# Fifteen weight blocks of a layer's input projection by Strassen's scheme (seven products of quarter blocks) in float32 sums

## The chip, the cores and the metric

The kernel runs on one core of a Trainium2 chip. Its engines are TensorE (PE; its weight loads, PEld, run beside its matmuls), VectorE (DVE), ScalarE (ACT), GpSimd (POOL) and SyncE (SP, which issues the DMA transfers). Each engine works through its own list of instructions in order. The metric is the device time of one execution in microseconds.

## The reference

One decoder layer on 1024 tokens of width 1024, all in float32, and a final norm:

```
h = rms_norm(x, norm_w);  proj = h @ w_in
z, xbc, dt_raw, pool_u, pool_gate, qkv, sb_gate, merge = split(proj)
y_ssm  = mamba2_branch(z, silu(causal_dwconv(xbc)), dt_raw, ...) @ w_proj_ssm
y_pool = pool_branch(pool_u, pool_gate, ...) @ w_proj_pool
y_sb   = stick_breaking_branch(qkv, sb_gate) @ w_proj_sb
x = x + (sum of sigmoid(merge_i) * y_i) @ w_out;  return rms_norm(x, final_norm_w)
```

## The kernel before, in words

Everything rests on products of h with blocks of 256 weight columns. A float32 operand is split into two float32r parts, `hi` (a cast, on ScalarE) and `lo` (the rest, a subtraction on Vector), and a product is three matmuls: hi·hi, hi·lo and lo·hi. A block in the transposed form (`gemm_b`, L148) is 2 column tiles of 128 times 2 token halves of 512, each 8 k-tiles times 3 matmuls of 512 columns: 96 matmuls. In the token form (`gemm_a`, L157) it is 8 token tiles times 24 matmuls of 256 columns. `hT[k]` holds the hi and lo of h's k-th tile for all 1024 tokens. `PLAN` is the order in which the blocks' weights are loaded (`load_half`, two 512 KB halves, through two `raw` buffers) and split (`split_half`).

`conv_part` is the first phase. Block ("x", 0) is computed while h is normed and transposed; ("x", b) for b up to 9 feeds the causal convolution: ScalarE writes the first tap from PSUM to `cacc` (L442), Vector adds three more taps from PSUM (L447), ScalarE takes a sigmoid (L450), GpSimd multiplies (L451), and a DMA stores the result. ("z", 0) with the dt columns follows ("x", 1); the short chain of dt (L378 to L418) is spread over the blocks after it. Then come ("g", 0) to ("g", 2), a SiLU gate for attention.

`attention_part` runs 64 units (8 head pairs, 2 heads, 4 pairs of query tiles). A unit's scores go PE, ACT (two sigmoids), DVE (scan L610, product L611), PE (transposes), ACT and DVE (split), PE (`av`). Between a unit's steps, TensorE is given fill: weight blocks of later work from the list `ATT_FILL`, spread over a pair's units by `share`. For six of the eight pairs the fill is three blocks: `vz` and `qk` of the next pair and one more (("g", 3), ("z", 1) to ("z", 3), ("m", 0), ("m", 1)); the first and the last pair have two. `merge_gen` (("m", i)) only copies its product out. The order of PE is written out by hand in attention, and that of PE, DVE, POOL and ACT in the first phase: there an engine that waits holds up all that stands behind it in the program. The scan, pool and merge phases follow.

## Time and profile before

| what | us |
|---|---|
| median of 3 runs (2081.27 to 2083.81) | 2081.63 |
| the profiled execution | 2080.79 |
| its span | 2079.0 |
| PE busy in the span | 2048.6 |
| DVE, ACT, POOL busy | 1203.2, 904.6, 348.9 |

The profiled execution's own time is its span and what lies around it (1.79 us). Busy time is the union of an engine's instructions, with matmul ends modelled; the share of an engine that does not bound a stretch says little about it.

### The profile page before, as it was taken

Reading aid. Unit: us, or ns where it says so; the run is one execution under the profiler, and the core shown is the slowest. Engines: PE = TensorE matmul, PEld = TensorE weight load, DVE = VectorE, ACT = ScalarE, POOL = GpSimd, SP = SyncE. Lnnn points to the kernel's source line nnn. Section 1 sums busy time; section 2 is a strip of 40 time slices with the busy share of each in tenths; the row PEclk is TensorE's granted clock in tenths of the full one; section 3 lists DMA queues with packets and bytes.
Section 4 is the critical chain, followed back from the end, with each engine's and each line's share of the span. In section 5 each row is a group of like instructions: output and inputs, shape, how many; then the busy total and the mean of one; then the engine's idle time right before and its main releaser. Section 6 shows DMA issues by size and latency. Waiting matters only on the chain.

```text
span 2079.0 us, 29567 instructions
## 1 busy us (share of the span) xinstructions
PE 2048.6 (99%) x11480; PEld 1751.9 (84%) x11480; DVE 1203.2 (58%) x1635; ACT 904.6 (44%) x1841; POOL 348.9 (17%) x415
## 2 busy tenths in 40 slices
PE   8999999999999999999999999999999999999998
PEld 6988889979899998888877877788888888888898
DVE  6466632676666776766774777773545424425333
ACT  5243322555555555555555666763322323323131
POOL 3112200021111111111112344430000002221000
PEclk9999999999999999999999999999999999999999
DMA  4323232112121212212215566654222625433232
GB/s 155 110 94 104 101 104 92 44 54 75 48 72 47 67 57 62 72 41 79 59 51 172 187 203 198 208 163 146 86 76 78 218 96 189 149 101 109 81 133 82
DMA packets 111677, 221.49 MB, mean 107 GB/s; under 512 B 9393, under 2 KB 59313, under 8 KB 111537
## 3 DMA queue, kind: packets, MB, share of 16 engines
q1 hardware_dynamic: 111536, 219.60, 32.4%
q8 instruction: 91, 1.49, 0.3%
q14 instruction: 50, 0.40, 0.1%
HBM read 162.15 MB, written 57.41 MB: 106 GB/s over the span
## 4 chain that ended last, share of the span: by engine, by line
PE 92%; DVE 4%; ACT 2%; issue 1%; DMA 1%; POOL 0%; SPq 0%; DVEq 0%; POOLq 0%; ACTq 0%
PE mm L148 34%; PE mmx L148 24%; PE mm L157 13%; PE mmx L157 4%; PE av L651 3%; PE yd L874 3%; PE tr L628 2%; DVE om L610 2%; PE z L601 1%; PE z L602 1%; PE yo L877 1%; PE st L880 1%; PE pp L755 1%; DVE be L611 1%; PE xp L858 1%
## 5 line engine op out<-in xcount | busy, mean ns | idle before, releaser
L148 PE MATMUL mm<-hT,w 128*128 128x512 f32 x2808 | 717.7, 401 | 3.1 <-DVE hT L345 2.8
L148 PEld LDWEIGHTS mm<-hT,w 128*128 128x128 f32 x2808 | 510.8, 188 | 115.6 <-issue 15.3
L129 DVE TENSOR_TENSOR w<-raw,w 128x1024 fp32r<-128x1024 f32 x142 | 207.7, 1463 | 149.6 <-ACT w L128 149.3
L157 PE MATMUL mm<-w,hT 128*128 128x256 f32 x2112 | 283.9, 286 | 1.2 <-ACT qb L545 1.2
L148 PE MATMUL mmx<-hT,w 128*128 128x512 f32 x1224 | 281.5, 389 | 0.0
L148 PEld LDWEIGHTS mmx<-hT,w 128*128 128x128 f32 x1224 | 229.7, 188 | 47.7
L157 PEld LDWEIGHTS mm<-w,hT 128*128 128x128 f32 x2112 | 263.4, 191 | 2.2 <-ACT qb L545 1.7
L148 PE MATMUL mmx<-x,w 128*128 128x512 f32 x1008 | 230.9, 389 | 0.0
L148 PEld LDWEIGHTS mmx<-x,w 128*128 128x128 f32 x1008 | 189.2, 188 | 39.3
L610 DVE TENSOR_TENSOR_SCAN om<-om,zero 128x128 f32<-128x128 f32 (+7 forms) x128 | 174.4, 1363 | 69.6 <-ACT om L605 69.0
L128 ACT CAST w<-raw 128x1024 fp32r<-128x1024 f32 x142 | 148.6, 1049 | 65.8 <-PE mmx L148 32.3
L630 ACT CAST attT<-tr 128x512 fp32r<-128x512 f32 (+2 forms) x224 | 98.4, 439 | 147.0 <-PE tr L628 79.3
L631 DVE TENSOR_TENSOR attT<-tr,attT 128x512 fp32r<-128x512 f32 (+2 forms) x224 | 111.0, 496 | 76.1 <-ACT attT L630 74.1
L605 ACT ACTIVATE om<-z 128x128 f32<-128x128 f32 (+2 forms) x192 | 92.8, 495 | 78.3 <-PE z L604 75.7
L148 PE MATMUL mm<-x,w 128*128 128x512 f32 x528 | 122.5, 390 | 0.0
L148 PEld LDWEIGHTS mm<-x,w 128*128 128x128 f32 x528 | 98.8, 188 | 21.5 <-ACT x L978 0.7
L1002 ACT ACTIVATE gt<-gt 128x1024 f32<-128x1024 f32 x32 | 34.0, 1062 | 184.0 <-DMA gt<-d_gate 181.3
L851 POOL TENSOR_TENSOR E<-E,cbm 128x1024 f32<-128x1024 f32 x32 | 76.3, 2385 | 161.4 <-issue 121.9
L611 DVE TENSOR_TENSOR be<-be,om 128x128 f32<-128x128 f32 (+7 forms) x128 | 96.9, 757 | 10.4
L1011 POOL TENSOR_TENSOR acc<-acc,gt 128x512 f32<-128x512 f32 x32 | 45.9, 1435 | 293.0 <-DVE gt L1010 293.0
L608 ACT ACTIVATE be<-z 128x128 f32<-128x128 f32 (+2 forms) x192 | 93.0, 498 | 0.1
L628 PE MATMUL tr<-cm,be 128*128 128x128 f32 x576 | 89.5, 273 | 0.5 <-DVE be L611 0.5
(194 smaller groups left out, 2515.6 us busy)
## 6 DMA issues: line engine op xcount, KB each, us to landing
raw<-in_wblk SPq DMA_DIRECT2D x148, 512.0 KB, 3.9
E<-d_act SPq DMA_DIRECT2D x32, 512.0 KB, 4.3
gt<-d_gate SPq DMA_DIRECT2D x32, 512.0 KB, 3.8
d_gate<-mg SPq DMA_DIRECT2D x24, 512.0 KB, 3.4
d_x<-csg SPq DMA_DIRECT2D x16, 512.0 KB, 2.7
xi<-d_x SPq DMA_DIRECT2D x32, 256.0 KB, 3.2
zs<-d_z SPq DMA_DIRECT2D x32, 256.0 KB, 2.8
d_ssm<-yt SPq DMA_DIRECT2D x32, 256.0 KB, 3.1
```

The lines of the kernel that those rows point to most:

```text
L128: nc.scalar.copy(hi, raw)
L129: nc.vector.tensor_tensor(out=lo, in0=raw, in1=hi.bitcast(F32), op=ALU.subtract)
L148: T.matmul(ps, w(a, k, ct * P, ct * P + P), mov(b, k, half * 512, half * 512 + 512), start=n == 0, stop=n == 23)
L157: T.matmul(ps, sta(a, k, tok * P, tok * P + P), w(b, k, 0, ncol), start=n == 0, stop=n == 23)
L605: A.activation(om[:, c0 : c0 + n], z[:, 0:n], AF.Sigmoid, scale=-0.125)
L608: A.activation(be[:, c0 : c0 + n], z[:, 0:n], AF.Sigmoid, scale=0.125)
L610: V.tensor_tensor_scan(out=rev, data0=rev, data1=self.zero.broadcast_to((P, L)), initial=1.0, op0=ALU.mult, op1=ALU.add)
L611: V.tensor_tensor(out=be[:, 0:L], in0=be[:, 0:L], in1=om[:, 1 : L + 1], op=ALU.mult)
L628: T.transpose(tr[:, c : c + P], b[:, (2 * jc + j) * P : (2 * jc + j + 1) * P], self.ident)
L630: A.copy(at[:, 0, sl], tr[:, sl])
L631: V.tensor_tensor(out=at[:, 1, sl], in0=tr[:, sl], in1=at[:, 0, sl].bitcast(F32), op=ALU.subtract)
L851: G.tensor_tensor(out=E, in0=E, in1=cbm[:, hg // 2].unsqueeze(1).broadcast_to((P, 8, P)), op=ALU.mult)
```

## The change

For fifteen blocks (`SEVEN`: x3 to x9, g0 to g3, m0 to m3) the product of the 1024 x 256 block A (transposed) with h is taken as a 2 x 2 product of quarters: A's halves over k and over columns, h's halves over k and over tokens. Winograd's form of Strassen's scheme needs seven quarter products, four sums of weight quarters (s1 to s4, per block, on GpSimd) and four of h (t1 to t4, once, on GpSimd and Vector, kept in `tt` and, for t1, in the upper token half of `hT[0]` to `hT[3]`, whose old content is parked in DRAM and brought back at the end), and seven sums of products. A quarter product is 4 k-tiles times 3 matmuls: 84 matmuls in a block for 96. Products five to seven are accumulated onto the PSUM banks of products one, three and four.

("g", 3) and ("m", 0) to ("m", 3) move from the fill of attention to the first phase; five pairs keep two fill blocks, the fourth gets ("z", 1), the last ("z", 2) and ("z", 3). ("z", 0) moves ahead of ("x", 1). The convolution of x3 to x9 reads SBUF, not PSUM, and stands in the next block's steps (`before`), as the gate of g0 to g3 does; the splits of the next block's quarters (`seven_prep`) stand there too.

```diff
-    extra = [("g", 3)] + [("z", i) for i in range(1, 4)] + [("m", i) for i in range(4)]
     order = [[("vz", p + 1), ("qk", p + 1)] for p in range(7)]
-    for p in range(1, 7):
-        order[p].insert(0, extra.pop(0))
-    return order + [extra]
+    order[3].insert(0, ("z", 1))
+    return order + [[("z", 2), ("z", 3)]]
+
+SEVEN = [("x", 3), ("g", 0), ("x", 4), ("m", 0), ("x", 5), ("g", 1), ("x", 6), ("m", 1), ("x", 7), ("g", 2), ("x", 8), ("m", 2), ("x", 9), ("g", 3), ("m", 3)]
...
+    for i in range(3):
         part(("x", i), OFF_X + 256 * i)
-        if i == 1:
+        if i == 0:
             part(("z", 0), OFF_Z + 1024)
-    for i in range(3):
-        part(("g", i), OFF_SG + 256 * i)
+    for kind, i in SEVEN:
+        part((kind, i), {"x": OFF_X, "g": OFF_SG, "m": OFF_M}[kind] + 256 * i)
...
+    def seven_prep(self, b):
+
+        nc = self.nc
+        G, A, V = nc.gpsimd, nc.scalar, nc.vector
+        assert self.wnext == 2 * b
+        self.wnext += 2
+        r0, r1 = (self.raw.pop(2 * b + i).rearrange("p (a b) -> p a b", b=256) for i in range(2))
+        a11, a21, a12, a22 = r0[:, :, 0:P], r0[:, :, P:256], r1[:, :, 0:P], r1[:, :, P:256]
+        t0 = self.wpool.tile([P, 2, 4, 256], F32R, tag="w", name=f"w{2 * b}")
+        t1 = self.wpool.tile([P, 2, 4, 256], F32R, tag="w", name=f"w{2 * b + 1}")
+        t2 = self.wspool.tile([P, 2, 4, 384], F32R, tag="ws", name=f"ws{b}")
+        s1, s2, s3, s4 = (self.s32pool.tile([P, 4, P], F32, tag="s32", name=f"s{i}", bufs=4) for i in range(4))
+        self.wseven[b] = {
+            "a11": lambda a, k: t0[:, a, k, 0:P],
+            "s2": lambda a, k: t0[:, a, k, P:256],
+            "s3": lambda a, k: t1[:, a, k, 0:P],
+            "s1": lambda a, k: t1[:, a, k, P:256],
+            "a12": lambda a, k: t2[:, a, k, 0:P],
+            "a22": lambda a, k: t2[:, a, k, P:256],
+            "s4": lambda a, k: t2[:, a, k, 256:384],
+        }
+
+        def split(t, c0, c1, src):
+            A.copy(t[:, 0, :, c0:c1], src)
+            V.tensor_tensor(out=t[:, 1, :, c0:c1], in0=src, in1=t[:, 0, :, c0:c1].bitcast(F32), op=ALU.subtract)
+
+        G.tensor_tensor(out=s1, in0=a21, in1=a22, op=ALU.add)
+        G.tensor_tensor(out=s2, in0=s1, in1=a11, op=ALU.subtract)
+        G.tensor_tensor(out=s3, in0=a11, in1=a21, op=ALU.subtract)
+        G.tensor_tensor(out=s4, in0=a12, in1=s2, op=ALU.subtract)
+        split(t0, 0, P, a11)
+        yield
+        split(t2, 0, 256, r1)
+        self.load_half()
+        self.load_half()
+        yield
+        split(t0, P, 256, s2)
+        yield
+        split(t1, 0, P, s3)
+        yield
+        split(t1, P, 256, s1)
+        yield
+        split(t2, 256, 384, s4)
+
...
+    def seven_operands(self, pool):
+
+
+        nc = self.nc
+        G, V = nc.gpsimd, nc.vector
+        self.tt = {i: pool.tile([P, 2, 4, 512], F32R, name=f"tt{i}") for i in (2, 3, 4)}
+        self.park = self.dram.tile([P, 4, 2, 512], F32, name="d_b12")
+        self.t1 = []
+        lo, hi = slice(0, 512), slice(512, 1024)
+        f = lambda t, part, sl: t[:, part, sl].bitcast(F32)
+
+        def tmp(name):
+            return self.s32pool.tile([P, 512], F32, tag="s32", name=name, bufs=4)
+
+        for k in range(4):
+            a, c = self.hT[k], self.hT[4 + k]
+            nc.sync.dma_start(out=self.park[:, k], in_=a[:, :, hi].bitcast(F32))
+            t1 = pool.tile([P, 512], F32, name=f"t1_{k}")
+            d, e = tmp("td"), tmp("te")
+            G.tensor_tensor(out=d, in0=f(a, 0, hi), in1=f(a, 0, lo), op=ALU.subtract)
+            G.tensor_tensor(out=t1, in0=f(a, 1, hi), in1=f(a, 1, lo), op=ALU.subtract)
+            V.tensor_tensor(out=t1, in0=t1, in1=d, op=ALU.add)
+            self.t1.append(t1)
+            G.tensor_tensor(out=e, in0=f(c, 0, hi), in1=t1, op=ALU.subtract)
+            V.tensor_tensor(out=e, in0=e, in1=f(c, 1, hi), op=ALU.add)
+            self.t_split(2, k, e)
+            yield
+            d = tmp("td")
+            G.tensor_tensor(out=d, in0=f(c, 0, lo), in1=e, op=ALU.subtract)
+            V.tensor_tensor(out=d, in0=d, in1=f(c, 1, lo), op=ALU.add)
+            self.t_split(4, k, d)
+            d, e = tmp("td"), tmp("te")
+            G.tensor_tensor(out=d, in0=f(c, 0, hi), in1=f(a, 0, hi), op=ALU.subtract)
+            G.tensor_tensor(out=e, in0=f(c, 1, hi), in1=f(a, 1, hi), op=ALU.subtract)
+            V.tensor_tensor(out=d, in0=d, in1=e, op=ALU.add)
+            self.t_split(3, k, d)
+            yield
+
+    def t_split(self, i, k, src):
+        hi, lo = self.tt[i][:, 0, k], self.tt[i][:, 1, k]
+        self.nc.scalar.copy(hi, src)
+        self.nc.vector.tensor_tensor(out=lo, in0=src, in1=hi.bitcast(F32), op=ALU.subtract)
+
+    def seven_first(self):
+
+        nc = self.nc
+        for k in range(4):
+            hi, lo = (self.hT[k][:, i, 512:1024] for i in range(2))
+            nc.scalar.copy(hi, self.t1[k])
+            nc.vector.tensor_tensor(out=lo, in0=self.t1[k], in1=hi.bitcast(F32), op=ALU.subtract)
+
+    def seven_last(self):
+        for k in range(4):
+            self.nc.sync.dma_start(out=self.hT[k][:, :, 512:1024].bitcast(F32), in_=self.park[:, k])
+
...
+    def seven_block(self, name, before, prep):
+
+        nc = self.nc
+        A, V, T = nc.scalar, nc.vector, nc.tensor
+        w = self.wseven.pop(BLK[name])
+        h = self.hT
+        mov = {
+            "b11": lambda b, k: h[k][:, b, 0:512],
+            "b21": lambda b, k: h[4 + k][:, b, 0:512],
+            "b22": lambda b, k: h[4 + k][:, b, 512:1024],
+            "t1": lambda b, k: h[k][:, b, 512:1024],
+            "t2": lambda b, k: self.tt[2][:, b, k],
+            "t3": lambda b, k: self.tt[3][:, b, k],
+            "t4": lambda b, k: self.tt[4][:, b, k],
+        }
+
+        def product(ps, a, b, first):
+            n = 0
+            for k in range(4):
+                for i, j in ((0, 0), (0, 1), (1, 0)):
+                    T.matmul(ps, w[a](i, k), mov[b](j, k), start=first and n == 0, stop=n == 11, skip_group_check=not first)
+                    n += 1
+
+        def step(i):
+            for f in before.get(i, ()):
+                f()
+            next(prep, None)
+
+        def add(out, ps, other):
+            V.tensor_tensor(out=out, in0=ps, in1=other, op=ALU.add)
+
+        c = [self.c_pool.tile([P, S + 4], F32, tag="cacc", name="cx") for _ in range(2)]
+        q = lambda i, j: c[i][:, 3 + 512 * j : 515 + 512 * j]
+        pu = self.stage("pu")
+        p1, u2, u3 = pu[:, 0:512], pu[:, 512:1024], q(0, 1)
+        x = self.mm()
+        product(x, "a11", "b11", True)
+        A.copy(p1, x)
+        step(0)
+        y = self.mm()
+        product(y, "s2", "t2", True)
+        add(u2, y, p1)
+        step(1)
+        z = self.mm()
+        product(z, "s3", "t3", True)
+        add(u3, z, u2)
+        step(2)
+        v = self.mm()
+        product(v, "s1", "t1", True)
+        add(q(1, 1), v, u3)
+        step(3)
+        product(x, "a12", "b21", False)
+        A.copy(q(0, 0), x)
+        step(4)
+        product(z, "a22", "t4", False)
+        add(q(1, 0), z, u2)
+        step(5)
+        product(v, "s4", "b22", False)
+        add(q(0, 1), v, u2)
+        step(6)
+        return c
+
...
+    def seven_x(self, b, c):
+
+        nc = self.nc
+        accs = []
+
+        def first():
+            for ct in range(2):
+                col = 2 * b + ct
+                nc.gpsimd.memset(c[ct][:, 0:3], 0.0)
+                acc = self.c_pool.tile([P, S], F32, tag="csg", name="acc", bufs=2)
+                cw = lambda k: self.conv_w[:, col, k : k + 1]
+                nc.scalar.activation(acc, c[ct][:, 3 : 3 + S], AF.Identity, scale=cw(3), bias=self.conv_b[:, col : col + 1])
+                for k in range(3):
+                    nc.vector.scalar_tensor_tensor(acc, c[ct][:, k : k + S], cw(k), acc, op0=ALU.mult, op1=ALU.add)
+                accs.append(acc)
+
+        def second(ct):
+            col = 2 * b + ct
+            sg = c[ct][:, 0:S]
+            nc.scalar.activation(sg, accs[ct], AF.Sigmoid)
+            nc.gpsimd.tensor_tensor(out=sg, in0=sg, in1=accs[ct], op=ALU.mult)
+            dst = self.d_x[col // 4][:, col % 4] if col < 16 else self.d_bc[:, col - 16]
+            nc.sync.dma_start(out=dst, in_=sg)
+
+        return {0: [first], 2: [lambda: second(0)], 3: [lambda: second(1)]}
+
...
+            self.zd = self.sb(zctx, "zd_sb", 1).tile([P, 2, 8, 288], F32R, name="zd")
             norm = self.norm_in(self.sb(nctx, "n_sb", 3), pps)
             for _ in range(3):
                 next(norm)
+            self.drain(self.conv_gen(0, pool, norm))
+            nctx.close()
+            self.zd_open(dpool)
             dt = self.dt_part(dpool)
-            for b in range(10):
-                self.drain(self.conv_gen(b, pool, norm if b == 0 else None))
-                if b == 0:
-                    nctx.close()
-                    self.zd_open(ctx, dpool)
-                else:
-                    next(dt, None)
-            for b in range(3):
-                self.drain(self.g_gen(b))
+            next(dt)
+            zctx.close()
+            tpool = self.sb(ctx, "t_sb", 1, "right")
+            self.s32pool = self.sb(ctx, "s32_sb", 1, "right")
+            sums = self.seven_operands(tpool)
+            for i, _ in enumerate(self.conv_gen(1, pool)):
+                next(sums, None)
+                if i > 1:
+                    next(sums, None)
+                if i % 2:
+                    next(dt)
+            self.wseven = {}
+            for i, _ in enumerate(self.conv_gen(2, pool)):
+                next(sums, None)
+                if i == 1:
+                    self.drain(sums)
+                    self.drain(dt)
+                    dctx.close()
+                    self.wspool = self.sb(ctx, "ws_sb", 2)
+                    prep = self.seven_prep(BLK[SEVEN[0]])
...
+
+            def halves():
+                for _ in range(2):
+                    self.split_half()
+                    yield
+
+            before = {}
+            for i, (kind, b) in enumerate(SEVEN):
+                prep = self.seven_prep(BLK[SEVEN[i + 1]]) if i + 1 < len(SEVEN) else halves()
+                before = make[kind](b, self.seven_block((kind, b), before, prep))
+            for i in sorted(before):
+                for f in before[i]:
+                    f()
+            self.seven_last()
         self.dump("bc", self.d_bc)
```

On GpSimd, in the first phase before, only the 20 multiplications of the convolution stand between the weight splits of the start and attention:

```order
L126 TENSOR_TENSOR w_426<-raw_215,w_426 128x512 x2
L126 TENSOR_TENSOR w_437<-raw_222,w_437 128x512 x2
L451 TENSOR_TENSOR csg<-csg,cacc 128x1024 x20
L592 MEMSET om 128x1 x2
L625 MEMSET attT 128x2x128
```

Now, during ("x", 1), the sums of h for the second, and then the third, pair of k-tiles stand between them (td, te: scratch; t_1, t_2: t1's tiles; of the trunk `csg` one row is left here):

```order
L213 TENSOR_TENSOR td<-hT_103 128x512
L214 TENSOR_TENSOR t_1_926<-hT_103 128x512
L217 TENSOR_TENSOR te<-hT_107,t_1_926 128x512
L222 TENSOR_TENSOR td<-hT_107,te 128x512
L226 TENSOR_TENSOR td<-hT_107,hT_103 128x512
L227 TENSOR_TENSOR te<-hT_107,hT_103 128x512
L663 TENSOR_TENSOR csg<-csg,cacc 128x1024
L213 TENSOR_TENSOR td<-hT_104 128x512
L214 TENSOR_TENSOR t_2_982<-hT_104 128x512
L217 TENSOR_TENSOR te<-hT_108,t_2_982 128x512
L222 TENSOR_TENSOR td<-hT_108,te 128x512
L226 TENSOR_TENSOR td<-hT_108,hT_104 128x512
```

Each of these sums stands between steps of Vector and ScalarE that it waits for or that wait for it, and the multiplication of `csg` (L663) stands in the same list. On Vector, an x block before was a split, and three taps from PSUM after each product:

```order
L129 TENSOR_TENSOR w_1064<-raw_910,w_1064 128x1024
L430 COPY cacc<-cols 128x3
L447 SCALAR_TENSOR_TENSOR cacc<-mm,cols,cacc 128x512 x3
L447 SCALAR_TENSOR_TENSOR cacc<-mm,cols,cacc 128x510
L447 SCALAR_TENSOR_TENSOR cacc<-mm,cols,cacc 128x511
L447 SCALAR_TENSOR_TENSOR cacc<-mm,cols,cacc 128x512
```

Now the six taps of an x block (L324, SBUF to SBUF) stand at the start of the next block's list, ahead of its splits (L174) and its sums of products (L278; pu and cx on the left are u2, then u3 and the four quarters):

```order
L324 SCALAR_TENSOR_TENSOR acc<-cx,cols,acc 128x1024 x6
L174 TENSOR_TENSOR w_1649<-raw_1537,w_1649 128x4x128
L278 TENSOR_TENSOR pu<-mmx,pu 128x512
L174 TENSOR_TENSOR ws_1651<-raw_1539,ws_1651 128x4x256
L278 TENSOR_TENSOR cx<-mmx,pu 128x512
L174 TENSOR_TENSOR w_1649<-s_1653,w_1649 128x4x128
L278 TENSOR_TENSOR cx<-mmx,cx 128x512
L174 TENSOR_TENSOR w_1650<-s_1654,w_1650 128x4x128
L174 TENSOR_TENSOR w_1650<-s_1652,w_1650 128x4x128
L278 TENSOR_TENSOR cx<-mmx,pu 128x512
L174 TENSOR_TENSOR ws_1651<-s_1655,ws_1651 128x4x128
L278 TENSOR_TENSOR cx<-mmx,pu 128x512
```

The sums of products, which PSUM banks wait for, moved behind the taps and between the splits. On TensorE the dt product, which stood behind ("x", 3):

```order
L148 MATMUL mmx<-hT_108,w_978 128x512 x3
L148 MATMUL mmx<-hT_109,w_978 128x512 x3
L400 MATMUL mmx<-adt,cm 128x256
L404 MATMUL mm<-adt,cm 128x256
L148 MATMUL mm<-hT_102,w_1064 128x512 x3
L148 MATMUL mm<-hT_103,w_1064 128x512 x3
```

now stands right behind ("x", 1), two blocks sooner after the product that it comes from:

```order
L361 MATMUL mm<-hT_109,w_582 128x512 x3
L610 MATMUL mm<-adt,cm 128x256
L616 MATMUL mmx<-adt,ones 128x256
L361 MATMUL mmx<-hT_102,w_774 128x512 x3
L361 MATMUL mmx<-hT_103,w_774 128x512 x3
```

## Rows read from the trace of the kernel before

**Rows 1.** The page, part 1: busy us, share of the span, instructions.
```profile
PE 2048.6 (99%) x11480; PEld 1751.9 (84%) x11480; DVE 1203.2 (58%) x1635; ACT 904.6 (44%) x1841; POOL 348.9 (17%) x415
```

**Rows 2.** Chain that ended last, in order: start us, us, what.
```profile
37.24 16.36 PE mmx L148 x72
...
336.10 23.03 PE mm L157 x192
359.13 21.79 PE mm L148 x96
```

**Rows 3.** Timeline of 48 to 52.5 us, Vector and GpSimd: start us, us, what.
```profile
48.39 2.42 POOL L451 TENSOR_TENSOR csg<-csg,cacc 128x1024 f32<-128x1024 f32 x1 [3.55 <-ACT csg L450]
49.02 2.32 DVE L447 SCALAR_TENSOR_TENSOR cacc<-mmx,cols,cacc 128x510 f32<-128x510 f32 x3 [3.13 <-ACT cacc L442]
...
51.25 0.28 DVE L357 CAST zd<-wdt_raw 128x256 fp32r<-128x256 f32 x1
...
51.57 0.42 DVE L358 TENSOR_TENSOR zd<-wdt_raw,zd 128x256 fp32r<-128x256 f32 x1
```

**Rows 4.** Timeline of 118 to 165 us, a convolution stretch.
```profile
121.96 1.28 ACT L380 ACT_TABLE_LOAD   x1
...
125.43 1.75 DVE L388 RECIPROCAL dt_w<-dt_w 128x256 f32<-128x256 f32 x1 [0.33 <-ACT dt_ln L384]
...
150.48 1.23 DVE L129 TENSOR_TENSOR w<-raw,w 128x1024 fp32r<-128x1024 f32 x1 [0.51 <-ACT w L128]
...
158.99 2.40 POOL L451 TENSOR_TENSOR csg<-csg,cacc 128x1024 f32<-128x1024 f32 x1 [9.84 <-ACT csg L450]
...
159.83 2.65 DVE L129 TENSOR_TENSOR w<-raw,w 128x1024 fp32r<-128x1024 f32 x1 [3.31 <-ACT w L128]
```

**Rows 5.** Timeline of 1225 to 1262 us, GpSimd, a scan stretch.
```profile
1223.70 2.38 POOL L851 TENSOR_TENSOR E<-E,cbm 128x1024 f32<-128x1024 f32 x1 [4.41 <-issue]
1226.03 1.50 POOL L886 TENSOR_TENSOR S<-S,dt_all 128x512 f32<-128x512 f32 x1
```

**Rows 6.** The same stretch, Vector.
```profile
1225.83 0.80 DVE L887 TENSOR_TENSOR y<-y,xk 128x512 f32<-128x512 f32 x1
```

**Rows 7.** Groups by line and form: line, engine, names, shapes, count | busy us, mean ns | idle.
```profile
L781 ACT COPY mg<-mm 128x512 f32<-128x512 f32 x48 | 28.0, 584 | 38.4 <-PE mm L148 38.2
L447 DVE SCALAR_TENSOR_TENSOR cacc<-mm,cols,cacc 128x512 f32<-128x512 f32 x36 | 27.0, 750 | 5.0 <-ACT cacc L442 3.7
...
L450 ACT ACTIVATE csg<-cacc 128x1024 f32<-128x1024 f32 x20 | 21.2, 1062 | 47.1 <-DVE cacc L447 29.7 <-DVE cacc L430 17.4
...
L442 ACT ACTIVATE cacc<-mmx,cols 128x509 f32<-128x509 f32 x14 | 10.9, 776 | 45.6 <-PE mmx L148 45.5
...
L1016 DVE TENSOR_TENSOR mg<-acc,mg 128x512 fp32r<-128x512 f32 x16 | 10.3, 687 | 5.3 <-ACT mg L1015 5.3
...
L734 DVE SCALAR_TENSOR_TENSOR u<-s,u 128x1024 f32<-128x1024 f32 x8 | 9.8, 1226 | 0.3
```

**Rows 8.** Timeline of 1728 to 1746 us, GpSimd.
```profile
1729.12 1.29 POOL L1011 TENSOR_TENSOR acc<-acc,gt 128x512 f32<-128x512 f32 x1 [1.54 <-DVE gt L1010]
```

**Rows 9.** Busy us (instructions) of each engine in two stretches of attention.
```profile
core 0: us, PE busy (x) PEld busy (x) DVE busy (x) ACT busy (x) POOL busy (x), PEclk, DMA share, GB/s
...
870.20:966.40 96.20, 95.19 (x601) 83.31 (x600) 65.37 (x91) 51.72 (x114) 13.69 (x32) 1.00 0.20 61
...
1055.40:1091.20 35.80, 33.60 (x191) 27.41 (x191) 26.48 (x35) 20.22 (x45) 5.37 (x15) 1.00 0.23 71
```

**Rows 10.** Of these stretches, the matmuls of line 148 alone.
```profile
1055.40:1091.20 35.80, 23.05 (x82) 13.95 (x82) 1.00 0.23 71
```

**Rows 11.** The same columns with the granted clock (PEclk), 540 to 556 us.
```profile
540.00:548.00 8.00, 6.77 (x36) 5.34 (x35) 7.35 (x7) 4.81 (x9) 1.73 (x5) 1.00 0.01 3
548.00:552.00 4.00, 3.29 (x18) 3.09 (x18) 3.32 (x5) 2.94 (x6) 1.28 (x1) 0.68 0.53 154
552.00:556.00 4.00, 4.00 (x33) 3.92 (x33) 2.10 (x5) 1.54 (x5) 0.10 (x1) 0.89 0.59 174
```

More of the change, by code (lines that the diff above doesn't have):

```diff
@@ L131, in split_half, with limit @@
         self.load_half()
+    def limit(self):
+        b = self.wnext // 2
+        while b < len(PLAN) and PLAN[b][0] not in SEVEN:
+            b += 1
+        return 2 * b
     def block(self, name):
         b = BLK[name]
-        while self.wnext < min(2 * b + (3 if b else 2), 2 * len(PLAN)):
+        while self.wnext < min(2 * b + (3 if b else 2), self.limit()):
             self.split_half()
@@ new lines, in seven_g, with part, seven_m @@
+    def seven_g(self, b, c):
+        nc = self.nc
+        def part(ct):
+            sg = self.c_pool.tile([P, S], F32, tag="csg", name="gsg", bufs=2)
+            nc.scalar.activation(sg, c[ct][:, 3 : 3 + S], AF.Sigmoid)
+            nc.gpsimd.tensor_tensor(out=sg, in0=sg, in1=c[ct][:, 3 : 3 + S], op=ALU.mult)
+            nc.sync.dma_start(out=self.d_g[:, 2 * b + ct], in_=sg)
+        return {0: [lambda: part(0)], 2: [lambda: part(1)]}
+    def seven_m(self, b, c):
+        def part(ct):
+            col = 2 * b + ct
+            self.nc.sync.dma_start(out=self.d_gate[col // 8][:, col % 8], in_=c[ct][:, 3 : 3 + S])
+        return {0: [lambda: part(0), lambda: part(1)]}
@@ L270, in constants @@
         nc, c = self.nc, self.const
-        cm = c.tile([P, 3, P], F32, name="cm")
+        cm = c.tile([P, 2, P], F32, name="cm")
         nc.sync.dma_start(out=cm, in_=self.ins["cmat"])
-        self.ident, self.tri, self.ones = cm[:, 0], cm[:, 1], cm[:, 2]
+        self.ident, self.tri = cm[:, 0], cm[:, 1]
         cols = c.tile([P, 132], F32, name="cols")
@@ L287, in constants @@
         self.dt_bias, self.a_log, self.d_skip = rows[:, 0:32], rows[:, 32:64], rows[:, 64:96]
-        self.inv = c.tile([P, 4, 16], F32, name="inv")
-        nc.sync.dma_start(out=self.inv, in_=self.ins["inv"])
         yield
@@ L403, in dt_part @@
         pt = self.mm()[:, 0:256].rearrange("p (a b) -> p a b", b=NH)
-        nc.tensor.matmul(pt.rearrange("p a b -> p (a b)"), self.ones, adf, start=True, stop=True)
+        ones = pool.tile([P, P], F32, name="ones")
+        nc.gpsimd.memset(ones, 1.0)
+        nc.tensor.matmul(pt.rearrange("p a b -> p (a b)"), ones, adf, start=True, stop=True)
         A.activation(self.cd, pt, AF.Exp)
@@ L448, in conv_gen @@
             if half == 1:
-                sg = pool.tile([P, S], F32, tag="csg", name="csg")
+                sg = pool.tile([P, S], F32, tag="csg", name="csg", bufs=2)
                 nc.scalar.activation(sg, acc[:, 0:S], AF.Sigmoid)
@@ L458, in conv_part @@
             ctx.enter_context(self.tc.manual_schedule(engines={mybir.EngineType.PE, mybir.EngineType.DVE, mybir.EngineType.Pool, mybir.EngineType.Activation}))
-            pool = self.sb(ctx, "c_sb", 3, "right")
-            dpool = self.sb(ctx, "dt_sb", 1, "right")
-            self.ps_extra(ctx, "c_ps", 3)
-            pps = self.ps(ctx, "n_ps", 3)
-            wz = pool.tile([P, 512], BF16, name="wz", bufs=1)
+            pool = self.c_pool = self.sb(ctx, "c_sb", 3, "right")
+            plain = ExitStack()
+            self.ps_extra(plain, "c_ps", 3)
+            pps = self.ps(plain, "n_ps", 3)
+            wz = pool.tile([P, S], F32, tag="csg", name="wz", bufs=2).bitcast(BF16)[:, 0:512]
             self.nc.gpsimd.memset(wz, 0.0)
@@ L703, in pool_part @@
             ppw = self.ps(ctx, "p_pw", 2)
+            self.inv = pool.tile([P, 4, 16], F32, name="inv", bufs=1)
+            nc.sync.dma_start(out=self.inv, in_=self.ins["inv"])
             parts = {}
@@ L1063, in host_arrays @@
     tri = np.triu(np.ones((P, P), np.float32))
-    cmat = np.stack([np.eye(P, dtype=np.float32), tri, np.ones((P, P), np.float32)], axis=1)
+    cmat = np.stack([np.eye(P, dtype=np.float32), tri], axis=1)
     import ml_dtypes
```

23 lines of the change are left out of this document (15 added, 8 removed).

## The prediction

> **What bounds the kernel now.** I read the page first: TensorE is busy for 2048.6 of 2079.0 us [rows 1], so the kernel is bound by its matmuls and a saved matmul is worth its spacing. The chain in order gives that: x0's last 48 and x1's first 24 matmuls of 512 columns take 16.36 us, and a block of 96 takes 21.79 us, 0.227 us each [rows 2]. Vector, at 58%, is not the bound in the mean, so what it can do in one stretch had to be read there: the first phase from timelines [rows 3, 4], attention from its busy time by stretch [rows 9]. What the reader is to see in these: where TensorE has cover, and how long the hand-offs between Vector, ScalarE and GpSimd take.
>
> **What is removed.** 15 blocks lose 12 matmuls each: 180 × 0.227 = **−40.9 us**, for certain. Blocks that only move between phases keep their matmul time.
>
> **What Vector and GpSimd do to each other.** The change puts GpSimd sums and two-operand Vector work on SBUF side by side everywhere, so this is priced first. A weight split on Vector (L129) takes 1.23 us alone and 2.65 us when a GpSimd multiplication (158.99 to 161.39) runs: it ends 1.09 us after GpSimd does [rows 4]. In the scan stretch Vector's L887 stretches to 0.80 us and ends 0.55 us after GpSimd's E; GpSimd's next instruction takes 1.50 us [rows 5, 6]. So two SBUF operands on Vector and a GpSimd operation run in turn, and whoever stands first goes first. Taps from PSUM do not mind: three take 2.32 us, 0.77 each, beside a GpSimd multiplication [rows 3]. Other prices: a GpSimd sum of 512 columns 1.29 us [rows 8], a multiplication of 1024 2.40 [rows 4], a Vector split of 512 0.69, a tap of 1024 from SBUF 1.23, a ScalarE copy 0.58, an activation of 1024 1.06, one from PSUM 0.78 [rows 7].
>
> **The block after an x block.** Count from its first matmul; a product is 12 × 0.227 = 2.72 us. ScalarE copies p1 until 3.35 and writes the first tap until 4.41 (it stands behind p1, in order). Vector's taps then run 1.23 each. After the third (8.2) ScalarE's sigmoid takes until 9.3 and GpSimd multiplies from 9.4 to 11.8: Vector's fifth tap, due at 9.4, starts at 11.7 and the sixth ends at 14.2. Then, in the order shown, the a11 split to 14.9, the sum u2 to 15.5 and the r1 split, which the second multiplication (15.4 to 17.7) holds up until 18.9; the sum u3 ends at 19.5. Product six accumulates in the bank that u3 reads, and TensorE is done with product five at 13.6: it stands for **6.0 us**. Behind it nothing more waits. The block takes 25.0 us, not 19.0; 21.8 before. It happens after each of the seven x blocks: **+42 us**. The other eight blocks have no taps, and Vector keeps up. Lower bound: without the turns, u3 would end at 15.0: 1.4 us, +10. Upper bound: +45, if all four sums of the next block also fall among the taps.
>
> No row before shows a tap with two SBUF operands beside GpSimd. The Trainium skill, SBUF — State Buffer, "Who interferes with whom", says that a Vector instruction with two SBUF inputs contends with a GpSimd one that reads SBUF, and that the loser blocks for the whole instruction. By that rule the taps are held as the split in rows 4 is, and the sum is the 42 us above; if taps ran free, as those from PSUM do, each of the seven waits would be 3.6 us, 25 in all. The trace agrees with the rule for splits and products; for such taps no run here shows it.
>
> **Before the first of the fifteen.** Count from the first matmul of x1. TensorE needs 21.8 us for x1, as much for x2, 1 for dt. The lists, walked in order with the prices above and 1.28 us a table load, 1.75 the reciprocal of dt [rows 4], come to this:
> - Vector takes x1's first taps until 8.7, the first k's t1 and t2 until 12.8, the second taps until 15.2. GpSimd's multiplication of csg stands next in its list, until 18.8; the first k's t4 and t3 end at 27.5. The dt chain (two table loads, the reciprocal) ends at 33.6. TensorE has stood at the dt product (L610) since 21.8: 11.8 us.
> - w7's split and taps until 37.2, the second k until 47.6, taps until 50.0, then in a row a table load, a sigmoid and GpSimd's multiplication (4.7) until 54.9. The third k takes 14.7: six GpSimd sums at 1.29, seven Vector steps at 0.69 in turns, and two casts that nothing covers. Then the copy that the dt transposes (L626) wait for: 69.9. TensorE has stood since 45.1: 24.9 us.
> - x2's taps and the fourth k until 94.4, with another 4.7 for csg inside; the first block's a11 split ends at 96.4. TensorE was done with x2 at 81.3: 15.1 us.
> - Its s2 split, behind more taps, costs 2.8 us; t1, written last, at 111.9, costs 4.6.
>
> Sum: **+59 us**. Put otherwise: in this stretch Vector has some 53 us of work and GpSimd 43, but each sum waits for the other's last one, so that they take 112 us together where TensorE offers 52.7. Lower bound: without the turns at the port the same walk gives +45; upper: 0.06 us more for each of some 100 hand-offs, +65.
>
> Ahead of that, z0 now follows x0 at once. x0 ends at 37.24 + 48 × 0.227 = 48.1 [rows 2]; the dt columns of z0's weights, which its first matmul reads, are split at 52.0 [rows 3], behind x0's last taps in Vector's list. x1 was the cover, which is gone: **+3.9 us**.
>
> The weights' loads are not in the way: two halves are asked for once the r1 split is done, and the walk leaves 6 us or more until the next sums. The park and its return, 2 MB each way on SP's queue, lie beside x0's end and beside the first half of vz0, which reads the lower tokens only: 0.
>
> **Attention.** With three blocks a pair takes 96.2 us [rows 9]: fill 21.79 × 2 + 23.03 = 66.6 [rows 2], so 29.6 of its own, and TensorE idles 1.0. Five pairs now have 44.8 + 29.6 = 74.4 us of matmuls, 37.2 a head, but Vector keeps its 65.4 less two splits, 62.9: 85%. The trace has one head with two blocks in its pair (1055.4 to 1091.2): Vector is busy for 26.48 of 35.8 us, 74%, and TensorE idles 2.2 [rows 9]; its fill is 82 matmuls, 18.6 us [rows 10]. At 85% it should idle more. If Vector's time out of work (9.3 us a head there) stays, a head takes 31.5 + 9.3 = 40.8, 3.6 late. I take 3.0, nearer to that: ten heads 30, less the 1.0 that each pair idles already: **+25 us**. Bounds: 2.2 a head, +17; 6.6 (out of work for 12.3 us, half way to the 15.4 of the three-block pairs), +61.
>
> **The clock.** After idle stretches of 1.2 and 0.7 us within 12, the granted clock was 0.68 and then 0.89 over 8 us [rows 11]: 4 × 0.32 + 4 × 0.11 = 1.7 us lost. Seven waits of 6 us at the x blocks, and the last of the early ones, fall as I think to that level: 8 × 1.7 = **+14 us**. Bounds: 0, and 38 if after each of the seven two products ran at 1.2 GHz.
>
> **Sum.** −40.9 + 42 + 59 + 3.9 + 25 + 14 = +103.0. On the profiled execution's own 2080.8 that is 2183.8; the median lies 0.8 higher: **2184.6 us**. A measurement here tells about 0.2%, 4 us, from no change.
>
> **The rivals.**
> - Hand-offs overlap (faster). Vector and GpSimd get through their work at the rate of the busier one, so that the early stretch is late only by its 53 us against 43.6 of x1 and x2, some 10, and no x block waits. Then −40.9 + 3.9 + 10 + 17 (attention at 2.2 a head) = −10: 2072. For it: the engines' sums do fit. Against it: the lists name each other's results in turn, with one scratch set. It decides if the dt product stands for less than 3 us and the whole early wait is under 20. Chance 0.05.
> - The port is not shared by these strided forms: early 45, x blocks 10, clock 2, attention 25, z0 3.9: 2127. Against it: rows 4 to 6. Chance 0.15.
> - Attention becomes Vector's: +61 there: 2220. For it: 85%. Against it: the head at 74% idles only 2.2. Chance 0.15.
> - My forecast 0.60; the rest 0.05, above these, where early waits and the clock meet their upper bounds.
>
> **How the numbers follow.** All lower bounds together give 2081.6 + 30 = 2112, all upper ones 2253; both at once are unlikely. The range takes in the second and third rivals about: 2122 to 2226, leaving out the first, half of the last, and a tail of the second. The likeliest case alone is 2155 to 2210. Faster by over 0.2%: 0.05. Within: 0.02. Slower: 0.93, all other cases.
>
> **What would show it.** The steps are right if PE has 180 instructions less in 512 columns and the same spacing; if PE stands at L610, L626 and the first L269 for some 12, 25 and 15 us; if each of seven blocks shows one wait of about 6 us on L278's u3, with taps of 1.23 us stretched to 3.6 beside GpSimd's L331; if PE's idle in attention grows to some 30 us, on Vector's L657 and L611; and if the clock dips below 1.00 after each. I am wrong in the early sum if PE waits under 40 us before the first L269, in the turns if taps keep 1.23 us beside L331, in attention if a two-block pair takes under 77 us or over 85.

## The result, and the profile after

The changed kernel takes 2190.2 us (median of 4 runs, 2188.8 to 2194.2) against 2082.5: a ratio of 1.052, 95% interval 1.050 to 1.054. The profiled execution took 2194.2 us with a span of 2192.4, 113.4 more than before.

The page's first part, and the granted clock from its second:

```profile
span 2192.4 us, 29585 instructions
PE 2050.9 (94%) x11300; PEld 1742.3 (79%) x11300; DVE 1321.9 (60%) x1730; ACT 938.6 (43%) x1909; POOL 507.0 (23%) x522
PEclk9968999999999999999999999999999999999999
```

180 matmuls have gone, yet TensorE is busy 2.3 us longer than in [rows 1]: it worked more slowly. Its longest waits, from the list of waits of the whole span (total, times, longest):

```profile
PE av L901 <- DVE o L907: 36.9, 26, 3.2
PE mmx L616 <- POOL ones L615: 29.3, 1, 29.3
PE mmx L269 <- DVE cx L278: 26.2, 7, 3.8
PE mm L610 <- DVE cacc L642: 11.5, 1, 11.5
PE mm L269 <- ACT ws L173: 6.6, 1, 6.6
PE mmx L269 <- DVE hT L243: 4.9, 2, 4.2
PE mmx L370 <- DVE zd L567: 3.4, 1, 3.4
```

The forecast's terms beside what the two traces show, in us of span:

| term | forecast | trace | how the trace has it |
|---|---|---|---|
| 180 matmuls | -40.9 | -40.9 | count by 0.227 |
| z0's weights | +3.9 | +3.4 | L370 on L567 |
| before the first of the fifteen | +59 | +53.4 | L610, L616, first L269, t1, and 1.1 on L659 |
| after the x blocks | +42 | +26.2 | seven waits on L278 |
| attention, idle | +25 | +27.3 | 39.0 idle of 670.4, against 11.7 of 743.3 |
| clock | +14 | +34 | half of TensorE's busy time in stretches at 1.2 GHz, less that of before |
| not priced | 0 | +10 | the rest; 4.4 are matmuls that follow each other more slowly |
| sum | +103.0 | +113.4 | |

The forecast stands beside the profiled execution, which is the slowest of the four; the median lies 4.0 us under it.

The clock's 34 are 3.0 behind z0's wait, 7.0 around the early waits, 15.7 in the fifteen blocks, 6.8 in attention, 1.7 behind it. The stretch behind z0's wait, with the granted clock behind the busy times (0.50 is 1.2 GHz):

```profile
51.70:57.80 6.10, 6.06 (x24) 5.82 (x25) 2.98 (x2) 1.90 (x2) 2.37 (x1) 0.50 0.50 185
```

The slower matmuls: a block without a wait (278.64 to 298.00, first matmul to first matmul) takes 19.36 us, and 84 × 0.227 are 19.07. Three of its products, of twelve matmuls each:

```profile
289.72 2.88 PE L269 MATMUL mm<-hT,ws 128*128 128x512 f32 x12
292.44 2.97 PE L269 MATMUL mmx<-tt,ws 128*128 128x512 f32 x12
295.25 2.92 PE L269 MATMUL mmx<-hT,ws 128*128 128x512 f32 x12
```

The product on `hT` is followed after 2.72 us, 0.227 a matmul; the one on `tt` after 2.81, 0.234. All through the trace the 36 matmuls of a block that read `tt` stand 0.234 us apart (median), the others 0.227: some 0.25 us of the 0.29. Why, no run shows.

**A block after an x block**, by the timeline of this kernel (start, duration), and the taps of all such blocks (shortest, median, longest in ns):

```profile
256.43 5.77 PE L269 MATMUL mmx<-tt,w 128*128 128x512 f32 x24
258.44 9.98 DVE L324 SCALAR_TENSOR_TENSOR acc<-cx,cols,acc 128x1024 f32<-128x1024 f32 x6 [3.84 <-ACT acc L322]
263.62 2.39 POOL L331 TENSOR_TENSOR cx<-cx,acc 128x1024 f32<-128x1024 f32 x1 [5.82 <-ACT cx L330]
268.94 0.68 DVE L278 TENSOR_TENSOR pu<-mmx,pu 128x512 f32<-128x512 f32 x1
269.54 1.21 DVE L174 TENSOR_TENSOR ws<-raw,ws 128x1024 fp32r<-128x1024 f32 x1
269.65 3.35 POOL L331 TENSOR_TENSOR cx<-cx,acc 128x1024 f32<-128x1024 f32 x1 [3.63 <-ACT cx L330]
270.67 0.68 DVE L278 TENSOR_TENSOR cx<-mmx,pu 128x512 f32<-128x512 f32 x1
271.41 4.27 PE L269 MATMUL mmx<-tt,ws 128*128 128x512 f32 x12 [3.74 <-DVE cx L278]
275.48 3.33 PE L269 MATMUL mmx<-hT,ws 128*128 128x512 f32 x12
...
L324 DVE SCALAR_TENSOR_TENSOR acc<-cx,cols,acc x42: 1277/1285/3506, 213.0 to 489.2; 128x1024 f32<-128x1024 f32 x42
```

The block starts at 253.71. Six taps take 9.98 us: the one that meets the first multiplication lasts 3.5. The r1 split (269.54) begins 0.11 us before the second multiplication, which then lasts 3.35 instead of 2.39 (in all seven blocks 3.33 to 3.37); the sums L278, one operand of which is in PSUM, keep their 0.68 inside it. u3 ends 17.6 us after the block's start, the wait is 3.74, and the two products behind it (4.27 and 3.33 for twelve matmuls, 2.9 elsewhere) lose 1.8 more: the granted clock was at 1.2 GHz from 272.9 to 276.3.

**The early stage**, by the same view:

```profile
121.10 1.71 POOL L226 TENSOR_TENSOR td<-hT,hT 128x512 f32<-128x512 f32 x1
121.62 1.75 DVE L223 TENSOR_TENSOR td<-td,hT 128x512 f32<-128x512 f32 x1
122.78 1.71 POOL L227 TENSOR_TENSOR te<-hT,hT 128x512 f32<-128x512 f32 x1
...
143.65 0.99 DVE L235 TENSOR_TENSOR tt<-td,tt 128x512 fp32r<-128x512 f32 x1 [0.68 <-ACT tt L234]
144.04 0.19 POOL L615 MEMSET ones<- 128x128 f32 x1
144.29 1.22 PE L616 MATMUL mmx<-adt,ones 128*128 128x256 f32 x2 [29.31 <-POOL ones L615]
```

Sums of 1.29 and 0.69 us become 1.71 and 1.75 where they meet. TensorE waits for a memset of 0.19 us that stands behind the third k's sums in GpSimd's list.

**Attention**, the same view:

```profile
1117.77 0.59 ACT L906 COPY o<-av 64x512 f32<-64x512 f32 x1
1118.44 1.75 DVE L860 TENSOR_TENSOR_SCAN om<-om,zero 128x768 f32<-128x768 f32 x1
1120.11 0.65 DVE L907 TENSOR_TENSOR o<-o,av 64x512 f32<-64x512 f32 x1
1120.82 0.74 PE L901 MATMUL av<-attT,vb 128*128 128x256 f32 x4 [1.42 <-DVE o L907]
```

av has one bank, which comes free only when Vector has added o (L907), and L907 stands behind a scan.

### The profile page after: what moved, and what is told of

It reads as the page before. It is cut to its first block, busy times and chain, and to the rows that moved or that the text cites. A ratio compares the mean times of both kernels' runs of the same rounds, so it can differ in the third digit from the quotient of the medians.

```text
span 2192.4 us, 29585 instructions
## 1 busy us (share of the span) xinstructions
PE 2050.9 (94%) x11300; PEld 1742.3 (79%) x11300; DVE 1321.9 (60%) x1730; ACT 938.6 (43%) x1909; POOL 507.0 (23%) x522
## 4 chain that ended last, share of the span: by engine, by line
PE 63%; DVE 9%; ACT 3%; issue 1%; DMA 1%; POOL 0%; DVEq 0%; SPq 0%; POOLq 0%; ACTq 0%
PE mm L361 21%; PE mmx L361 15%; PE mm L370 9%; DVE om L860 5%; PE mmx L370 3%; PE av L901 3%; PE yd L1126 3%; DVE be L861 2%; PE tr L878 2%; ACT om L855 1%; PE yo L1129 1%; PE st L1132 1%; PE pp L1007 1%; DVE attT L881 1%; PE mmx L269 1%
## 5 line engine op out<-in xcount | busy, mean ns | idle before, releaser
L361 PE MATMUL mm<-hT,w 128*128 128x512 f32 x1920 | 504.7, 406 | 2.9 <-DVE hT L556 2.8
L361 PEld LDWEIGHTS mm<-hT,w 128*128 128x128 f32 x1920 | 349.9, 189 | 82.8 <-issue 15.3
L370 PE MATMUL mm<-w,hT 128*128 128x256 f32 x2112 | 296.0, 288 | 0.0
L370 PEld LDWEIGHTS mm<-w,hT 128*128 128x128 f32 x2112 | 268.8, 192 | 0.3
L129 DVE TENSOR_TENSOR w<-raw,w 128x1024 fp32r<-128x1024 f32 x114 | 154.8, 1359 | 111.1 <-ACT w L128 110.7
L361 PE MATMUL mmx<-hT,w 128*128 128x512 f32 x672 | 157.7, 394 | 0.0
L128 ACT CAST w<-raw 128x1024 fp32r<-128x1024 f32 x114 | 119.5, 1053 | 69.4 <-PE mmx L361 30.0
L361 PEld LDWEIGHTS mmx<-hT,w 128*128 128x128 f32 x672 | 127.7, 190 | 26.9
L842 POOL MEMSET om<- 128x1 f32 x128 | 12.5, 98 | 355.8 <-DVE be L861 325.1
```

Source lines behind the costliest of these rows:

```text
L128: nc.scalar.copy(hi, raw)
L129: nc.vector.tensor_tensor(out=lo, in0=raw, in1=hi.bitcast(F32), op=ALU.subtract)
L361: T.matmul(ps, w(a, k, ct * P, ct * P + P), mov(b, k, half * 512, half * 512 + 512), start=n == 0, stop=n == 23)
L370: T.matmul(ps, sta(a, k, tok * P, tok * P + P), w(b, k, 0, ncol), start=n == 0, stop=n == 23)
```

## The experiments

The theory: the loss is waits, each at a place where a short instruction stands behind others in an in-order list, or where Vector and GpSimd run in turn, and the clock lost behind them. The rivals: the amount of Vector's work; the memset alone; a cost of the new first phase in attention. The kernel before ran again beside each set of runs, with medians of 2080.7 to 2082.5 us, so a difference of 2 us between two sets says nothing.

**1. The ones set early.** `nc.gpsimd.memset(ones, 1.0)` stands ahead of z0.

> One edit: the memset of the tile of ones (L615) is written ahead of z0, so that it no longer stands behind the third k's sums in GpSimd's list. My theory: the early waits come from the hand-offs between Vector and GpSimd, and the memset is only the place where the second one shows. The 29.3 us at L616 go, but the copy of acum (L611) still stands behind the third k's sums on Vector, so TensorE gets through half of x2 (10.9 us) and one dt product and then stands some 17 to 24 us at the transposes, L626; the total falls by 0 to 10 us. Rival: the memset's place is the cause; the 29.3 us go for good, L626 does not wait, and the total falls by 25 to 33 us.

2188.4 us, no change. Waits of TensorE in the early stage:

```profile
PE mm L626 <- DVE dt_all L613: 20.4, 1, 20.4
PE mm L612 <- DVE cacc L642: 11.5, 1, 11.5
PE mm L269 <- ACT ws L173: 11.0, 1, 11.0
```

The 29.3 us go, and 24.8 come back: 20.4 at the transposes, where the forecast had put them, and 4.4 more at the first block (11.0 for 6.6). The memset was only the place.

**2. The taps apart.**

```diff
-        return {0: [first], 2: [lambda: second(0)], 3: [lambda: second(1)]}
+        return {0: [lambda: first([0])], 1: [lambda: second(0)], 2: [lambda: first([1])], 4: [lambda: second(1)]}
```

> One edit: in the block after an x block the second channel tile's three taps are issued after the sum u3 instead of ahead of it (its sigmoid and multiplication two steps later). My theory: product six waits only because six taps, one of them held by GpSimd's multiplication, stand ahead of u3 on Vector; so the seven waits on L278 (26.2 us) go nearly whole, and with them the clock lost in the block behind each (15.7 us in the fifteen): 35 to 42 us less than the changed kernel. Rival: Vector is full in these blocks (six taps 7.7, two holds 2.3 each, splits 4.7, sums 3.4: 20.4 us against 19.4 of products), so the wait comes back at product seven or at the next block's first product with 1 to 2 us each, and the gain is 15 to 25 us.

2173.3 us, 16.9 less: the rival had the size, and the place too. The waits on L278 are 14.2 us in eight, seven of them of 2.0 at product seven. By the timeline, u3 is in time, but the sum that product seven waits for now stands behind the second tile's taps:

```profile
261.11 0.68 DVE L278 TENSOR_TENSOR cx<-mmx,pu 128x512 f32<-128x512 f32 x1
261.70 3.91 DVE L324 SCALAR_TENSOR_TENSOR acc<-cx,cols,acc 128x1024 f32<-128x1024 f32 x3
266.13 0.69 DVE L278 TENSOR_TENSOR cx<-mmx,cx 128x512 f32<-128x512 f32 x1
266.88 1.43 PE L269 MATMUL mmx<-hT,ws 128*128 128x512 f32 x5 [1.98 <-DVE cx L278]
```

This run alone does not tell a full Vector from a place in the list. Run 7 speaks for the place: there these taps stand one step later, and the waits at the x blocks are 1.1 us at most.

**3. The multiplications on Vector.** `nc.vector` for `nc.gpsimd` in L331.

> One edit: after an x block the two multiplications sigmoid times sum (L331) run on Vector instead of GpSimd, at the same places of the list. My theory (Vector and GpSimd run in turn where both read SBUF): no tap is held, all 42 take 1.28 us, u3 ends 15.6 us after the block's start instead of 17.6, and product six waits 2.0 us instead of 3.74: 14 us in seven blocks instead of 26, though Vector has 2.5 us more work in each block. Rival (GpSimd is not what stretches a tap; Vector's amount of work alone counts): one tap of six still takes 3.5 us, and the waits stay at 3.7 us or grow.

2207.9 us, 17.7 more. The taps, and one block:

```profile
L324 DVE SCALAR_TENSOR_TENSOR acc<-cx,cols,acc x42: 1277/1285/1287, 211.0 to 499.4; 128x1024 f32<-128x1024 f32 x42
...
268.23 3.05 PE L269 MATMUL mmx<-tt,ws 128*128 128x512 f32 x12 [1.53 <-DVE cx L278]
274.29 0.69 DVE L278 TENSOR_TENSOR cx<-mmx,cx 128x512 f32<-128x512 f32 x1 [4.38 <-DMA d_x<-cx]
275.03 5.49 PE L269 MATMUL mmx<-hT,ws 128*128 128x512 f32 x12 [3.75 <-DVE cx L278]
```

Without GpSimd's multiplications no tap is held, and the wait for u3 falls to 1.53 (2.0 expected): turns, as the theory has it. The total grew by a wait that no theory had, so that the waits on L278 are 37.9 us in 14: the multiplication comes later, so its store does too, and the next sum writes the buffer (one of three of cx) that is being stored.

**4. Blocks moved, no seven products.** The kernel before with the changed `att_fill`, four g and four m blocks in the first phase, six buffers for V (`dynamic_dma_scratch_size=1024` makes room).

> The kernel before, without seven products: only g3 and m0 to m3 are moved out of attention into the first phase as plain blocks, z1 to z3 are put where the changed kernel has them, and the tiles of V get the changed kernel's six buffers. My theory: the loss in attention comes from the two-block pairs alone, whatever the first phase does: attention's TensorE idle grows from 11.7 to about 39 us as in the changed kernel, the clock adds 5 to 9, and the total is 2112 to 2122 us. Rival: part of attention's loss is brought by the new first phase (weights that come late, the park, the clock's state), so that here attention idles at most 25 us and the total stays under 2100.

2118.2 us, as the theory has it:

```profile
PE av L653 <- DVE o L659: 36.9, 26, 3.3
```

The same 36.9 us in 26 waits, with 38.8 of idle in attention: its loss comes from the move alone. The clock took 11.8 us there, above the 5 to 9 expected.

**5. The operand sums on Vector.** `G = V = nc.vector` in `seven_operands`.

> One edit: the operand sums of the first phase that GpSimd took (seven a k) run on Vector, at the same places of the list. My theory (the early waits are turns: each sum waits for the other engine's last one, and where both read SBUF they do not overlap): a k takes 13 Vector steps of 0.69 us and three uncovered casts, some 11 us, instead of 14.7, so TensorE's early waits fall from 53.5 us to 25 to 38, although Vector has 19 us more work. Rival (Vector's amount of work sets it): the early waits grow by 10 to 19 us, to 64 or more.

2177.7 us. Early waits 8.4, 20.2, 7.3 and 4.4, 40 us in all, 2 above my range. GpSimd's sums are six a k, 24 in all and not the 28 that the expectation reckons with: 16.6 us at 0.69. Vector's busy time grew by 10.3 (1321.9 to 1332.2), since GpSimd no longer holds its own steps, and TensorE waits 13 less. So Vector's amount is not what set the early waits. How much of the 13 is the turns, and how much GpSimd's longer sum (1.29) and the hand-offs, no run parts.

**6. Ten blocks.** `att_fill` of before; x3 g0 x4 g1 x5 g2 x6 x7 x8 x9.

> g3 and m0 to m3 go back into attention as plain blocks, at the places of the kernel before; ten blocks keep the seven products (x3 to x9, g0 to g2). My theory (attention pays for the two-block pairs, and every x block costs the same whatever follows it): attention idles 12 us again instead of 39 and gets its clock back (7), five blocks lose their saving (13.6 us); the seven waits stay at 3.7 us each; 2190 - 27 - 7 + 14 = 2170 us, 2164 to 2176. Rival: where an x block follows an x block (x6 to x9) Vector and GpSimd have no block to catch up in, the waits there double, and the total is 2177 to 2190.

2168.5 us, as the theory has it, in part by luck: the waits on the sums are 19.8 us in five, 4.8 the longest, less than the 26 expected, but x9 now stands right ahead of attention, and vz0 waits 9.9 us that it does not wait in the changed kernel: 3.7 for the split of its weights and 6.2 for what run 7 shows.

**7. Eight blocks.** x5 g0 x6 g1 x7 g2 x8 x9; plain x1 to x4; ones early; `first([1])` at step 3; GpSimd keeps the two sums of t3.

> What the runs so far point to, put together: attention filled as in the kernel before; eight blocks by seven products (x5 to x9, g0 to g2); the sums spread over four plain blocks x1 to x4 and run on Vector but for two a k; the ones set early and the dt products moved half a block later; the second tile's taps one more step behind u3 than in the run with the taps apart. My theory (the waits are places in lists and turns between two engines, not Vector's amount of work): early waits 3 to 12 us, x waits under 2 us each, removed 21.8, z0 +3.4, clock +2 to 6: 2068 to 2086 us. Rival (operand sums cost what they cost): the early waits stay above 25 us and the total is 2092 to 2110.

2125.7 us, outside both. The x waits are 1.1 at most, as hoped; the early waits still 26, now in ten places; and 12.6 us that nobody had, inside vz0, the first block behind the convolution:

```profile
359.56 1.46 SPq L258 DMA_DIRECT2D hT<-d_b  x3
...
382.49 3.93 DVE L335 SCALAR_TENSOR_TENSOR acc<-cx,cols,acc 128x1024 f32<-128x1024 f32 x3 [3.67 <-POOL cx L330]
387.55 0.41 ACT L774 CAST va<-mm 128x128 fp32r<-128x128 f32 x2
389.19 0.75 DVE L780 TENSOR_TENSOR zsg<-zsg,mm 128x256 f32<-128x256 f32 x2 [0.25 <-ACT zsg L779]
389.71 2.69 PE L381 MATMUL mm<-w,hT 128*128 128x256 f32 x11 [12.63 <-issue]
```

The parked halves (L258) had landed by 370.6, so it is not they that vz0's upper tokens wait for. Its two banks are full, and the instructions that empty the first (L774 to L780) stand in ScalarE's and Vector's lists behind the last x block's taps and sigmoids: TensorE goes on 0.10 us after the first of the two L780 ends. In runs 6 and 9 it goes on 0.10 us after the same instruction too.

**8. Two banks for av** in the changed kernel.

```diff
-            pz = self.ps(ctx, "a_z", 3)
+            pz = self.ps(ctx, "a_z", 2)
-            pav = self.ps(ctx, "a_av", 1)
+            pav = self.ps(ctx, "a_av", 2)
```

> The changed kernel with one edit in attention: the product av gets two banks of PSUM instead of one, and the scores z two instead of three (the eight banks are full). The forecast's reading (Vector is out of room in two-block pairs, at 85%): TensorE's idle in attention stays at 30 us or more, and only shifts from L907 to other waits on Vector. Rival (a hand-off: the one bank comes free only when Vector has added o, and o stands behind ScalarE's activations and a scan of up to 1.75 us in Vector's list): the 36.9 us on L907 fall under 10; with two banks z may wait up to 15 us in all on ScalarE's L855 and L858; the total falls by 20 to 40 us, to 2150 to 2170.

2155.7 us, 34.5 less, with the same work on Vector. Attention's waits, and its busy times (us, then PE, PEld, DVE, ACT, POOL, and the granted clock):

```profile
PE z L851 <- ACT be L858: 8.3, 14, 1.2
PE tr L878 <- DVE attT L881: 2.5, 4, 0.9
...
560.50:1195.80 635.30, 622.34 (x4360) 560.73 (x4358) 503.15 (x701) 374.09 (x857) 118.51 (x249) 1.00 0.20 56
```

Against the changed kernel:

```profile
565.00:1235.40 670.40, 631.36 (x4359) 566.98 (x4357) 502.83 (x701) 377.44 (x857) 115.46 (x249) 0.99 0.18 53
```

The rival holds: Vector does 503 us of work in either; it was the hand-off of one bank (TensorE idles 13.0 us for 39.0), and the clock behind it.

**9. Plain g blocks as cover.** Plain x1, g0, x2, g1; seven products for x3 to x9, then g2; `seven_last()` ahead of the last block's stores; z0's dt columns split during x0.

> The last but one run's kernel (eight blocks by seven products, attention as before) with four edits. Plain blocks are now x1, g0, x2, g1, since a plain g block leaves Vector 19 us of its 21.8 and an x block only 10; seven products for x3 to x9 and g2. The parked halves come back ahead of the last block's stores in SP's queue. The dt columns of z0's weights are loaded ahead of x0 and split in its third quarter. My theory (waits are places in lists): the 12.6 us at the boundary to attention and the 3.4 us of z0 go, early waits fall from 24 to under 10 us, x waits stay at 0.2 to 1.1 each, the clock loses under 8: 2064 to 2082 us, not slower than the kernel before. Rival: seven x blocks in a row are too much for Vector and GpSimd in turns (22.3 us of SBUF work in 19.4), so each loses 3 us, and the early waits stay above 15: 2095 to 2115 us.

2104.2 us: the rival's range. Early waits are 11 us, z0's none. The boundary to attention costs 1.8: the last block is now g2, which leaves less work ahead of vz0's first bank; the parked halves had been in time before. But the waits on the sums are 14.2 us in five, three of them of 3.7: x blocks in a row do need a block between them.

**10. Thirteen blocks**, alternating but for x3 x4, with two banks for av.

> Thirteen blocks by seven products (x3, x4, g2, x5, g3, x6, m0, x7, m1, x8, m2, x9, m3), the early part of the last kernel with plain x1, g0, x2, g1 (the dt products issued ahead of the sums in each quarter), attention's two-block pairs with two banks for av and two for z. My theory (what the change loses is places in lists and one bank, each of which can be taken away): removed 35.4 us, 0.3 us more a block for seven products' starts (4), early waits 4 to 10, x waits under 1.1 each where a block without taps follows, attention idles 13, clock under 6: 2060 to 2076 us, faster than the kernel before. Rival (seven products bring their own cost in sums on Vector and GpSimd that grows with the blocks): waits of 3.7 us stay at most x blocks and the early waits above 12: 2085 to 2105 us.

2080.8 us, ratio to before 0.9997 (0.9988 to 1.0006): between the two. Early waits are 10 us, and x4 after x3 waits 3.7.

**11. The control:** the kernel before with the edit of run 8 alone.

> The kernel before with only attention's banks changed: two for av, two for z. It is the control for the run with thirteen blocks. In the kernel before three-block pairs cover most of the hand-off (TensorE idles 11.7 us in attention, 9.5 of it on av), so my theory gives 0 to 9 us less, 2073 to 2082; the rival (z needs its third bank where the fill is longer too, 8 us of waits) gives no gain, 2080 to 2086.

2071.0 us, ratio 0.9954 (0.9941 to 0.9966), a little under my range. z does not miss its third bank: its waits are 0.9 us.

**12. Twelve blocks**, x3 plain ahead of g1.

> The kernel with thirteen blocks, but x3 is plain and stands ahead of g1, so that the sums have five plain blocks (x1, g0, x2, x3, g1) and a block without taps follows every x block by seven products; twelve blocks keep them. My theory (the thirteen lost 9.7 us in the early stage and 5.4 where x4 followed x3, and the clock 7 with them; each is a place in a list): removed 32.7 us, starts +4, other small waits and z0's place +5, early 2 to 5, x waits 0 to 3, clock 1 to 4, attention as in the kernel before: 2062 to 2071 us, faster than the kernel before by 0.5 to 0.9%. Rival (the sums take what they take wherever they stand): early waits and clock again above 12 us, 2076 us or more. Whether it is better than the kernel before with two banks (2071.0) is not settled by either if it comes out within 4 us of that.

2072.5 us, ratio 0.9960 (0.9947 to 0.9974), 1.5 above my range. Waits of its first phase:

```profile
PE mmx L277 <- DVE cx L286: 2.9, 3, 1.4
PE mmx L369 <- DVE cacc L668: 2.1, 1, 2.1
PE mm L369 <- DVE w L132: 2.0, 2, 1.3
PE mmx L369 <- DVE w L132: 1.9, 1, 1.9
```

It beats both kernels, but not the control, whose interval overlaps: 32.7 us of matmuls are saved and 33.5 spent again. By stages of the two traces: some 11 us in attention's two-block pairs, 10.6 of idle ahead of attention, 3.4 of clock, 9 in the slower matmuls on `tt` (some 3) and changes there that no run parts.

## Why the prediction was right, and where not

The time was right to 5.6 us, and it came that near partly by luck: the waits after the x blocks came 15.8 us short of their price, the clock cost 20 more than its own, and the two nearly cancel.

- **Removed, z0, t1, L610:** as forecast. (The dt product does not stand two blocks nearer to the product that it comes from, as the text on the change has it, but one: x2 and x3 were between them, now x1 alone. The walk had that right.)
- **Before the first of the fifteen:** 53.4 for 59. The waits are those of two lists that wait for each other (run 5), with turns in them: a sum of 0.69 lasts 1.75. The second wait showed at L616 rather than L626, since I had overlooked that the ones now come from GpSimd's list; run 1 shows that this moves the wait and does not make it. The first block's wait was 6.6 rather than 15.1: that part of the walk was too long.
- **After the x blocks:** mechanism right, size off: 3.74 each for 6.0. The step that failed is "the r1 split, which the second multiplication (15.4 to 17.7) holds up until 18.9": in the trace the split comes first by 0.11 us, ends 17.0 us after the block's start, and it is GpSimd that waits. Beware of the number: 3.74 is almost the 3.6 that the text gives for taps that run free, but the taps were held (3.5 us). The Trainium skill, SBUF — State Buffer, "Who interferes with whom", says that issue order decides who blocks, and that a Vector instruction with at most one SBUF input does not contend. The trace agrees on the held multiplication (3.35) and on the L278 sums (0.68). For the held taps (3.5) it does not show the order: in all seven blocks the tap starts 0.02 to 0.04 us ahead of the multiplication that holds it.
- **Attention:** +27.3 of idle for +25, but for another reason, so the size was luck. "If Vector's time out of work (9.3 us a head there) stays" was not the cause: with Vector's work unchanged, a second bank took the loss away (run 8), and the move alone brought it (run 4). The third rival, attention bound by Vector, falls with it.
- **Clock:** 34 for 14. I charged 1.7 us to eight waits. The seven waits of 3.74 cost 1.7 to 2.9 each, and z0's, the early ones and attention's, for which I had charged one dip in all, cost 3.0, 7.0 and 6.8.
- **Not priced:** matmuls on `tt` stand 0.234 us apart and not 0.227, most of 4.4 us in fifteen blocks. The terms "0.3 us more a block for seven products' starts" of run 10 and "starts +4" of run 12 are this.
- **A sum:** the lower bounds of the forecast add up to +35.0, 2117 us, not to the +30 and 2112 that it gives; the range does not rest on them.

What stays open: some 5 us of the unpriced 10, why matmuls on `tt` are slower, and what part of the early waits is the turns.
